# Order of work at six places of a hybrid transformer block on one core

## The chip, the core and the metric

The kernel runs on one core of a Trainium2 chip. The metric is the device time of one execution in microseconds, the median of three runs. All data are float32. PE is TensorE, DVE VectorE, ACT ScalarE, POOL GpSimd and SP SyncE, which only issues DMAs.

## The reference

One block of width 1024 over a sequence of 1024 tokens: a norm, a projection that feeds three mixers, an output projection with a residual, a second norm and a feed-forward part.

```python
h = rms_norm(x, attn_norm[l])
xa, qkv, z, b, a, c_q, c_kv, k_pe = jnp.split(h @ w_in[l], offsets, axis=-1)
y_a = pool_mixer(xa, pool_w[l], pool_scale[l])
y_b = gated_deltanet(qkv, z, b, a, dn_conv[l], dn_a_log[l], dn_dt_bias[l], dn_norm[l])
y_c = mla_attention(c_q, c_kv, k_pe, positions, ...)
x = x + jnp.concatenate([y_a, y_b, y_c], axis=-1) @ w_out[l]
h = rms_norm(x, mlp_norm[l])
x = x + jnp.square(jax.nn.relu(h @ w_up[l])) @ w_down[l]
```

`gated_deltanet` (4 heads of 128) solves, per chunk of 64 tokens, a unit lower triangular system and then carries a 128 x 128 state from chunk to chunk. `mla_attention` (4 heads) takes queries and keys from small latents, which are normed and rotated per token. `pool_mixer` takes moving means over 2 to 16 tokens.

## The kernel before

Every matmul is three (`mm3`, line 121): each operand is split into a high and a low part (`split`, line 113: ACT copies the high part, DVE or POOL subtracts), and high x high, high x low and low x high are added in PSUM. Tokens lie in eight tiles of 128 or two halves of 512.

The stages follow each other so:

- **First norms** (lines 196 to 260): eight x tiles are loaded, normed (`norm1`), transposed on PE (`turn`) and multiplied with a column group (`group`) that gives gates and latents. The weights of that group come in four loads (`load_g`) and are split by `split_g`. The order of SP is written by hand here; elsewhere a scheduler orders each engine's instructions by their place in the program and their dependences.
- **Column tiles** (`proj_tile`, line 480): the other columns of the projection in 18 tiles of 128, each in two halves of 24 matmuls. `tile_order` (line 473) is 6 to 9 (keys of the four heads), 0 and 1 (pool mixer), then per head query (2 to 5), value (10 to 13) and gate (14 to 17). `prefetch` loads and splits the next tile's weights. After each half, `pump(n, m)` (line 464) takes n steps of the generators in `side` and m of those in `slow`.
- Those generators are `latents()` (line 374: per token tile `latent_a`, `latent_b`, and `latent_c`, which norms and rotates), run during tiles 6 to 9; `lanes()` (line 575), the inverse of the triangular matrices in 31 steps of two DVE instructions, at high priority; `levels(h)`, which builds the larger blocks of the inverse with matmuls on PE after the small ones went through memory (`t_dram`); `chain(h)`, the state's way through the chunks of head h; and `pool(i, xa)`, the moving sums, on POOL.
- **Attention** (lines 990 to 1058): keys are loaded and transposed (`load_k`), then score, softmax and weighting pieces run while the chain of the last head ends: this beginning is the ramp.
- **Output projection** (`out_tile`, line 1088), per half of the tokens, with the squares for the second norm. `stats(hf)` (line 1112) sums them on PE, takes the reciprocal root on DVE, puts it on a diagonal (`dg`) and spreads it over the partitions with a matmul (line 1124).
- **Up part** (lines 1132 to 1413): a scheme of seven products (`products_12`, `product_6`, `products_rest`) for each of 16 pairs of weight blocks. `up_raw` loads the blocks, `halves` and `sums` combine them on POOL, `kept` combines the results and stores them in `u_dram`. Four pairs are begun early, during the output projection.
- **Down part** (`wave`, line 1359): seven products per group again, with `load_u`, `load_d`, `prepare`, and x loaded again from `x_dram`.

The last iteration over the pairs, where the up part turns into the down part, reads:

```python
        if last:
            kept(last, p - 1)
        if p == NFF // 2 - 1:
            load_u(0)
            load_u(1)
            load_d(0, 2, 0)
            acch = [S((P, 4, 1024), "H", 4)]
            prepare(0)
        products_rest(v, p)
        last = v
    kept(last, p)
```

## Time and profile before

| | us |
|---|---|
| runs | 1260.46, 1258.84, 1261.3 |
| profiled execution | 1258.98 |
| its span | 1257.3 |
| busy in the span: PE | 1178.5 (94%) |
| DVE | 851.7 (68%) |
| ACT | 575.0 (46%) |
| POOL | 260.9 (21%) |

The mean granted clock of PE is 0.972 of full speed. A span is from the first to the last instruction; an engine's busy time leaves out its waits. A window's row gives the same for a stretch of the span.

### The profile page before, as it was taken

Reading aid. Unit: us, or ns where it says so; the run is one execution under the profiler, and the core shown is the slowest. Engines: PE = TensorE matmul, PEld = TensorE weight load, DVE = VectorE, ACT = ScalarE, POOL = GpSimd, SP = SyncE. Lnnn points to the kernel's source line nnn. Section 1 sums busy time; section 2 is a strip of 40 time slices with the busy share of each in tenths; the row PEclk is TensorE's granted clock in tenths of the full one; section 3 lists DMA queues with packets and bytes.
Section 4 is the critical chain, followed back from the end, with each engine's and each line's share of the span. In section 5 each row is a group of like instructions: output and inputs, shape, how many; then the busy total and the mean of one; then the engine's idle time right before and its main releaser. Section 6 shows DMA issues by size and latency. Waiting matters only on the chain.

```text
span 1257.3 us, 16363 instructions
## 1 busy us (share of the span) xinstructions
PE 1178.5 (94%) x5802; PEld 965.9 (77%) x5802; DVE 851.7 (68%) x1692; ACT 575.0 (46%) x1187; POOL 260.9 (21%) x230
## 2 busy tenths in 40 slices
PE   5999996999999699997997999999997999999998
PEld 4968784788787578786876788888875888888887
DVE  7768779776657587538475556466457987786863
ACT  4655441554445477524264455555444333333330
POOL 3121023402020345243133323223210000000000
PEclk9999998999999699998999999999998999999999
DMA  6112222311101211571124443443489645442202
GB/s 251 35 51 89 92 89 84 109 33 29 36 24 55 89 34 35 188 248 66 42 76 167 167 162 124 176 150 136 176 318 382 207 163 167 151 135 93 100 27 101
DMA packets 84738, 152.62 MB, mean 121 GB/s; under 512 B 25520, under 2 KB 28720, under 8 KB 84656
## 3 DMA queue, kind: packets, MB, share of 16 engines
q1 hardware_dynamic: 74512, 140.03, 31.7%
q10 hardware_dynamic: 10144, 11.54, 2.7%
q8 instruction: 46, 0.75, 0.2%
q14 instruction: 36, 0.29, 0.1%
HBM read 105.41 MB, written 46.14 MB: 121 GB/s over the span
## 4 chain that ended last, share of the span: by engine, by line
PE 75%; DVE 12%; DMA 5%; ACT 3%; issue 2%; POOL 2%; SPq 0%; POOLq 0%; DVEq 0%; ACTq 0%
PE mm L1370 13%; PE mm L1154 11%; PE sm L1154 6%; PE sm L1370 5%; PE ch L1370 5%; PE mm L123 5%; PE mm L124 5%; PE mm L122 5%; PE ch L1154 2%; DMA upr<-in_w_up_dram 2%; PE sm L746 2%; PE ch L124 1%; DVE tl L587 1%; PE ch L122 1%; PE ch L123 1%
## 5 line engine op out<-in xcount | busy, mean ns | idle before, releaser
L1370 PE MATMUL mm<-dop,dop 128*128 128x512 f32 x768 | 180.2, 395 | 8.3 <-ACT dop L114 6.5
L1370 PEld LDWEIGHTS mm<-dop,dop 128*128 128x128 f32 x768 | 145.8, 190 | 40.8 <-ACT dop L114 7.3
L1154 PE MATMUL mm<-H,wop 128*128 128x512 f32 x576 | 137.4, 390 | 0.0
L1154 PEld LDWEIGHTS mm<-H,wop 128*128 128x128 f32 x576 | 107.9, 188 | 22.9 <-DVE wop L115 0.5
L114 ACT CAST dop<-wdr 128x1024 fp32r<-128x1024 f32 x48 | 50.4, 1049 | 164.0 <-PE ch L1370 69.8
L122 PE MATMUL mm<-H,w 128*128 128x512 f32 x288 | 117.4, 408 | 1.1 <-DVE t2k L501 1.1
L124 PE MATMUL mm<-H,w 128*128 128x512 f32 x288 | 116.5, 404 | 0.0
L123 PE MATMUL mm<-H,w 128*128 128x512 f32 x288 | 115.9, 402 | 0.0
L1154 PE MATMUL sm<-op,wop 128*128 128x512 f32 x384 | 94.9, 396 | 7.7 <-ACT wop L114 6.9
L1154 PEld LDWEIGHTS sm<-op,wop 128*128 128x128 f32 x384 | 72.7, 191 | 25.1 <-ACT wop L114 8.2
L115 POOL TENSOR_TENSOR w<-raw,w 128x1024 fp32r<-128x1024 f32 x18 | 43.8, 2431 | 229.4 <-ACT w L114 215.7
L115 DVE TENSOR_TENSOR dop<-wdr,dop 128x1024 fp32r<-128x1024 f32 x48 | 58.7, 1222 | 39.3 <-ACT dop L114 39.2
L1234 ACT ACTIVATE uo<-uo 128x512 f32<-128x512 f32 x48 | 30.3, 632 | 90.3 <-DVE uo L1212 46.0
L1370 PE MATMUL sm<-dop,dop 128*128 128x512 f32 x288 | 69.1, 395 | 2.4 <-ACT dop L114 2.0
L115 DVE TENSOR_TENSOR wop<-s,wop 128x512 fp32r<-128x512 f32 x64 | 47.6, 775 | 32.0 <-ACT wop L114 31.7
L115 DVE TENSOR_TENSOR dop<-H,dop 128x1024 fp32r<-128x1024 f32 x56 | 68.2, 1217 | 0.0
L1370 PE MATMUL ch<-dop,dop 128*128 128x512 f32 x288 | 67.8, 390 | 0.0
L1370 PEld LDWEIGHTS sm<-dop,dop 128*128 128x128 f32 x288 | 54.8, 191 | 14.7 <-ACT dop L114 2.5
L1370 PEld LDWEIGHTS ch<-dop,dop 128*128 128x128 f32 x288 | 54.2, 188 | 11.2
L122 PEld LDWEIGHTS mm<-H,w 128*128 128x128 f32 x288 | 54.8, 190 | 10.3 <-DVE t2k L501 1.5
L124 PEld LDWEIGHTS mm<-H,w 128*128 128x128 f32 x288 | 54.8, 190 | 9.4
L123 PEld LDWEIGHTS mm<-H,w 128*128 128x128 f32 x288 | 55.0, 191 | 9.0
(383 smaller groups left out, 2588.5 us busy)
## 6 DMA issues: line engine op xcount, KB each, us to landing
...
```

Of the source, the lines that this page charges most:

```text
L114: A.copy(hi, src)
L115: (eng or V).tensor_tensor(lo, src, f32(hi), op=ALU.subtract)
L122: PE.matmul(o, ah, bh, start=first, stop=False)
L123: PE.matmul(o, ah, bl, start=False, stop=False)
L124: PE.matmul(o, al, bh, start=False, stop=last)
L587: V.tensor_tensor(TL[:, j + 1:32, 0:m], TL[:, j + 1:32, 0:m], tv, op=ALU.subtract)
L746: PE.matmul(pa[:, c, :], lhs[:, c, :], rhs[:, c, :], start=True, stop=True)
L1154: PE.matmul(o, x_, y_, start=(first and j == 0 and q == 0), stop=(j == 3 and q == 2), skip_group_check=True)
L1234: A.activation(o, o, AF.Relu)
L1370: PE.matmul(o, x_[:, cs_], y_, start=(q in (0, 1, 3) and i == 0 and e == 0), stop=(i == GP - 1 and e == 2), skip_group_check=True)
```

## The change

- Start: all four weight loads come ahead of the second x tile, their splits are on DVE instead of POOL, and the norms of tiles 1 to 7 run in groups of two and three.
- Latents: the thirteen instructions of `latent_c` move from DVE to POOL, and `LAT` (steps per half) is 4.
- Column tiles: two gates come first, the mixer tiles last, with their second halves in `load_k` and in the ramp; a query's products with the keys stand between the halves of its value tile; three weight splits move to DVE.
- Norm statistics: `stats` ends with the reciprocal root; the diagonal and its matmul are `spread`, called one output tile later.
- Up part: each pair's blocks are loaded a pair ahead (`preload`).
- Turn: the first down weights and u blocks are loaded ahead of the kept stores; x is loaded again in four quarters by SP.

```diff
-LAT = 3
+LAT = 4
...
+SIDE = 9
...
     def load_g(q):
-        raw = wg_raw[q] = S((P, 2, NG), "raw", 3)
+        raw = wg_raw[q] = S((P, 2, NG), *(("raw", 3) if q < 3 else ("w", 4)))
         nc.sync.dma_start(raw, w_g[:, 2 * q:2 * q + 2, :])
 
     def split_g(q):
         wg_hi[q], wg_lo[q] = U((P, 2, NG), F32R, "wghi"), U((P, 2, NG), F32R, "wglo")
-        split(wg_hi[q], wg_lo[q], wg_raw.pop(q), G)
+        split(wg_hi[q], wg_lo[q], wg_raw.pop(q))
...
+    def norm1(*ts):
+        sl = slice(ts[0], ts[-1] + 1)
+        for t in ts:
+            A.activation(C((P, 1024), "lv", 3, BF16), xr[t], AF.Square, accum_out=ss1[:, t:t + 1])
...
+        for t in ts:
+            V.scalar_tensor_tensor(xr[t], xr[t], r1[:, t:t + 1], gbc, op0=ALU.mult, op1=ALU.mult)
...
@@ -225,31 +227,28 @@
     with tc.manual_schedule(engines={nc.sync.engine}):
         load_x()
         nc.sync.dma_start(gbc, attn_norm.broadcast_to([P, D]))
-        load_g(0)
+        for q in range(4):
+            load_g(q)
         load_x()
-        load_g(1)
-        load_g(2)
         load_x()
         norm1(0)
         split_g(0)
-        load_g(3)
+        split_g(1)
+        turn(0)
+        load_x()
         load_x()
         nc.sync.dma_start(par, params)
         nc.sync.dma_start(pos, positions)
-        turn(0)
-        split_g(1)
-        norm1(1)
         split_g(2)
         split_g(3)
         while len(xr) < NT:
             load_x()
-        for t in range(2, 1 + LEAD):
-            norm1(t)
         group(0)
+        norm1(1, 2)
         turn(1)
         for t in range(1, NT):
-            if t + LEAD < NT:
-                norm1(t + LEAD)
+            if t in (2, 4):
+                norm1(*range(t + 1, min(t + 4, NT) if t == 4 else t + 3))
...
         pe = C((P, 5, 32), "pe", 1)
-        V.tensor_tensor(pe[:, 0:4, :], q4[:, :, 64:96], rs[:, t, 4:8].unsqueeze(2).to_broadcast([P, 4, 32]), op=ALU.mult)
-        V.tensor_scalar(pe[:, 4, :], qk[:, 896:928], rs[:, t, 12:13], None, op0=ALU.mult)
-        V.tensor_tensor(pe, pe, pv("gpe").rearrange("p (a b) -> p a b", a=5), op=ALU.mult)
+        G.tensor_tensor(pe[:, 0:4, :], q4[:, :, 64:96], rs[:, t, 4:8].unsqueeze(2).to_broadcast([P, 4, 32]), op=ALU.mult)
+        G.tensor_scalar(pe[:, 4, :], qk[:, 896:928], rs[:, t, 12:13], None, op0=ALU.mult)
...
+        G.tensor_tensor(kn[:, :, 0:64], kv4[:, :, 0:64], rs[:, t, 8:12].unsqueeze(2).to_broadcast([P, 4, 64]), op=ALU.mult)
+        G.tensor_tensor(ro[:, :, 0:16], pe[:, :, 0:16], cb, op=ALU.mult)
+        G.tensor_tensor(ro[:, :, 16:32], pe[:, :, 16:32], cb, op=ALU.mult)
+        G.tensor_tensor(rt[:, :, 0:16], pe[:, :, 16:32], sb, op=ALU.mult)
+        G.tensor_tensor(rt[:, :, 16:32], pe[:, :, 0:16], sb, op=ALU.mult)
+        G.tensor_tensor(ro[:, :, 0:16], ro[:, :, 0:16], rt[:, :, 0:16], op=ALU.subtract)
+        G.tensor_tensor(ro[:, :, 16:32], ro[:, :, 16:32], rt[:, :, 16:32], op=ALU.add)
+        G.tensor_copy(qn[:, :, 64:96], ro[:, 0:4, :])
+        G.tensor_copy(kn[:, :, 64:96], ro[:, 4:5, :].to_broadcast([P, 4, 32]))
...
-    tile_order = [6, 7, 8, 9, 0, 1] + [b + h for h in range(H) for b in (2, 10, 14)]
+    tile_order = [6, 7, 8, 9, 14, 15, 2, 10, 3, 11, 4, 12, 16, 5, 13, 17, 0, 1]
...
-            loaded[ct] = load_w(w_tiles[ct], eng=G)
...
+            loaded[ct] = load_w(w_tiles[ct], eng=V if ct in (15, 2, 10) else G)
...
-
-    def conv_silu(ci, dst, after=None):
+            if between and hf == halves[0]:
+                between()
...
-    for i in range(2):
-        xa = U(s="xa")
+    XA = [None] * 2
+
+    def mixer(i):
+        xa = XA[i] = U(s="xa")
 
         def use_x(hf, pm):
             A.copy(xa[:, hf * 512:(hf + 1) * 512], pm)
 
-        proj_tile(i, use_x, 4, 3)
-        slow.append(pool(i, xa))
+        return i, use_x
...
+        proj_tile(2 + h, conv_silu(h, qt), SIDE)
+
+    def query_key(h):
+        qt = QT[h]
         transposed(qt, square_sums(ssq[:, h, :]))
...
     side.append(levels(0))
+    for h in range(2):
+        proj_tile(*gate(h), 8, 2)
     for h in range(H):
         queries(h)
-        v = values(h)
-        if h < H - 1:
-            proj_tile(*v, 6)
-            side.append(chain(h))
-            proj_tile(*gate(h), 6)
-        else:
-            z = gate(h)
-            proj_tile(*v, 6)
-            side.append(chain(h))
-            proj_tile(*z, 6, halves=(0,))
+        proj_tile(*values(h), SIDE, between=lambda: query_key(h))
+        side.append(chain(h))
+        if h > 1:
+            proj_tile(*gate(h), SIDE)
+    mix = [mixer(i) for i in range(2)]
+    for i in range(2):
+        proj_tile(*mix[i], SIDE, halves=(0,))
...
     for t in range(NT):
-        if t == 7:
-            proj_tile(*z, 6, halves=(1,), tag="mm")
+        if t == 0:
+            proj_tile(*mix[0], SIDE, halves=(1,))
+            slow.append(pool(0, XA[0]))
         load_k(t)
...
-    slow.append(pool_out(0))
-    slow.append(pool_out(1))
-    step(slow, 0)
+
+    def mixer_end():
+        proj_tile(*mix[1], 0, 0, halves=(1,), tag="ch")
+        slow.extend((pool(1, XA[1]), pool_out(0), pool_out(1)))
+        yield
...
+            if n == 0:
+                gens.append(mixer_end())
...
+    st = [None] * 2
+
     def stats(hf):
...
+        st[hf] = HM((P, 3, 4), s="st")
+        V.tensor_scalar(st[hf][:, 0, :], pt[:, :, 0], 1.0 / D, EPS, op0=ALU.mult, op1=ALU.add)
+        newton_rsqrt(st[hf][:, 1, :], st[hf][:, 0, :], st[hf][:, 2, :])
+
+    def spread(hf):
         dg = HM((P, 4, P), s="dg")
-        V.tensor_tensor(dg, ident.unsqueeze(1).to_broadcast([P, 4, P]), st[:, 1, :].unsqueeze(2).to_broadcast([P, 4, P]), op=ALU.mult)
+        V.tensor_tensor(dg, ident.unsqueeze(1).to_broadcast([P, 4, P]), st[hf][:, 1, :].unsqueeze(2).to_broadcast([P, 4, P]), op=ALU.mult)
         R[hf] = MM("ch")
         PE.matmul(R[hf], ones, dg.rearrange("p a b -> p (a b)"), start=True, stop=True)
...
+    raws = {}
+
+    def preload(p):
+        if p < NFF // 2 and p not in raws:
+            raws[p] = up_raw(p), up_raw(p + NFF // 2)
+
     def first_two(p):
         v = Pair()
-        v.r0 = up_raw(p)
+        preload(p)
+        v.r0 = raws[p][0]
         v.a11, v.a12 = w_op(v.r0[:, 0:4, :]), w_op(v.r0[:, 4:8, :])
...
             square(k, 1, n)
+            if n == 1:
+                spread(0)
...
-                    v.r0 = v.r1 = v.parts = v.s12 = None
+                    v.r0 = v.parts = v.s12 = None
                 else:
...
+        if p == 0:
+            spread(1)
     v0 = early_pairs[0]
     T2 = op_u()
...
+    raw_u = {}
+
     def load_u(n):
         g, q = divmod(n, 7)
-        if len(ur) < 2 and n % 2 == 0:
+        if n > 1 and len(ur) < 2 and n % 2 == 0:
             ur.append(S((P, 4, 2, 512), "H", 4))
         for h in range(2):
             p = GP * g + 2 * h
-            nc.sync.dma_start(ur[n // 2 % 2][:, 2 * (n % 2) + h], u_dram[q, p:p + 2].rearrange("a p t -> p a t"))
+            t_ = raw_u[n, h] = M((P, 2, 512), s="ur") if n < 2 else ur[(n // 2 - 1) % 2][:, 2 * (n % 2) + h]
+            nc.sync.dma_start(t_, u_dram[q, p:p + 2].rearrange("a p t -> p a t"))
+
+    def load_x(q):
+        hs = slice(512 * (q % 2), 512 * (q % 2) + 512)
+        nc.sync.dma_start(acch[q // 2][:, :, hs], x_dram[4 * (q // 2):4 * (q // 2) + 4, :, hs].rearrange("k p t -> p k t"))
...
             sums(v)
             products_12(v)
             product_6(v)
+        preload(p + 1)
+        if p == NFF // 2 - 1:
+            load_d(0, 2)
+            load_u(0)
+            load_d(0, 0)
+            load_u(1)
         if last:
             kept(last, p - 1)
         if p == NFF // 2 - 1:
-            load_u(0)
-            load_u(1)
-            load_d(0, 2, 0)
             acch = [S((P, 4, 1024), "H", 4)]
+            load_x(0)
             prepare(0)
         products_rest(v, p)
         last = v
+    load_d(0, 1, 3)
     kept(last, p)
+    acch.append(S((P, 4, 1024), "H", 4))
     load_u(2)
-    acch.append(S((P, 4, 1024), "H", 4))
-    for k in range(KD):
-        x2[k] = acch[k // 4][:, k % 4, :]
-        nc.scalar.dma_start(x2[k], x_dram[k])
-    load_d(0, 1, 3)
+    load_x(2)
     load_u(3)
+    load_x(3)
+    load_x(1)
     for n in range(n_wave):
         g, q = divmod(n, 7)
         if n + 1 < n_wave:
```

POOL, ahead of the inverse; `tl` is its start value, `w` a weight tile's low part, `nrm`, `ro` and `pe` belong to latents. Before:

```order
L115 TENSOR_TENSOR w_1792<-raw_1789,w_1791 128x1024
L115 TENSOR_TENSOR w_1959<-raw_1956,w_1958 128x1024
L578 MEMSET tl_1774 128x1024
L579 AFFINE_SELECT tl_1774<-tl_1774 128x1024
L115 TENSOR_TENSOR w_2061<-raw_2058,w_2060 128x1024
L115 TENSOR_TENSOR w_2265<-raw_2262,w_2264 128x1024
L115 TENSOR_TENSOR w_2435<-raw_2432,w_2434 128x1024
L621 COPY xs_1945<-xa_1696 128x1
L622 TENSOR_TENSOR xs_1945<-xa_1696 128x1023
```

With the change (line numbers are those of the changed kernel):

```order
L358 TENSOR_TENSOR nrm_1804<-qk_1625,rs 128x4x64
L359 TENSOR_TENSOR nrm_1804<-qk_1625,rs 128x4x64
L366 COPY nrm_1804<-ro_1805 128x4x32
L367 COPY nrm_1804<-ro_1805 128x4x32
L579 MEMSET tl_1819 128x1024
L580 AFFINE_SELECT tl_1819<-tl_1819 128x1024
L116 TENSOR_TENSOR w_2245<-raw_2242,w_2244 128x1024
L116 TENSOR_TENSOR w_2394<-raw_2391,w_2393 128x1024
```

The two rows of `tl` (memset and identity) came behind a weight split and ahead of three; now they come behind the last latent.

DVE, norm statistics of the first half; `st` is the reciprocal root, `dg` the diagonal, `wop<-s` the split of a summed weight block, `x<-mm` the residual addition of an output tile. Before:

```order
L115 TENSOR_TENSOR wop_6146<-upr_6141,wop_6146 128x512
L132 SCALAR_TENSOR_TENSOR st_5853<-st_5853 128x4
L133 SCALAR_TENSOR_TENSOR st_5853<-st_5853 128x4
L1122 TENSOR_TENSOR dg_5866<-ident,st_5853 128x512
L115 TENSOR_TENSOR wop_6154<-s_1193_6151,wop_6154 128x512
L1128 SCALAR_TENSOR_TENSOR x_1117_5544<-x_1117_5544,g_5525,ch_5868 128x512
L1128 SCALAR_TENSOR_TENSOR x_1118_5546<-x_1118_5546,g_5525,ch_5868 128x512
```

With the change (line numbers are those of the changed kernel):

```order
L116 TENSOR_TENSOR wop_6100<-upr_6093,wop_6100 128x512
L133 SCALAR_TENSOR_TENSOR st_5805<-st_5805 128x4
L134 SCALAR_TENSOR_TENSOR st_5805<-st_5805 128x4
L116 TENSOR_TENSOR wop_6106<-s_1193_6103,wop_6106 128x512
L1105 TENSOR_TENSOR x_1139_5676<-mm_5819,x_1139_5676 128x512
L1136 TENSOR_TENSOR dg_5849<-ident,st_5805 128x512
L1142 SCALAR_TENSOR_TENSOR x_1117_5496<-x_1117_5496,g_5477,ch_5851 128x512
```

The diagonal moved behind the split of a summed block and one residual addition.

SP's queue, first pairs of the up part; `upr` are weight blocks of pairs 1, 2, 3, `uo` and `t` results that are stored. Before:

```order
L1230 DMA u_dram<-uo_6307 128x512
L1230 DMA u_dram<-uo_6339 128x512
L1142 DMA upr_6545<-in_w_up_dram 128x1024
L1142 DMA upr_6547<-in_w_up_dram 128x1024
L1230 DMA u_dram<-uo_6499 128x512 x2
L1230 DMA u_dram<-t_1247_6567 128x512
L1230 DMA u_dram<-t_1248_6568 128x512
L1230 DMA u_dram<-t_1247_6567 128x512
L1230 DMA u_dram<-t_1248_6568 128x512
L1142 DMA upr_6640<-in_w_up_dram 128x1024
L1142 DMA upr_6642<-in_w_up_dram 128x1024
```

With the change (line numbers are those of the changed kernel):

```order
L1251 DMA u_dram<-uo_6259 128x512
L1156 DMA upr_6437<-in_w_up_dram 128x1024
L1251 DMA u_dram<-uo_6291 128x512
L1156 DMA upr_6439<-in_w_up_dram 128x1024
L1156 DMA upr_6519<-in_w_up_dram 128x1024
L1156 DMA upr_6521<-in_w_up_dram 128x1024
L1251 DMA u_dram<-uo_6455 128x512 x2
L1251 DMA u_dram<-t_1249_6523 128x512 x2
L1251 DMA u_dram<-t_1250_6524 128x512 x2
L1156 DMA upr_6614<-in_w_up_dram 128x1024
L1156 DMA upr_6616<-in_w_up_dram 128x1024
```

The blocks of the second of these pairs moved ahead of the six stores that follow, those of the third one group of stores up.

## Rows read from the trace of the kernel before

**Rows 1.** Waits of PE: engine, line, releaser: us in total, times, longest.
```profile
PE sm L519 <- DVE qt L509: 12.4, 1, 12.4
```

**Rows 2.** Windows: us, busy (instructions) of five engines, PEclk, DMA share, GB/s.
```profile
0.00:20.00 20.00, 4.86 (x14) 3.55 (x15) 12.60 (x34) 10.02 (x15) 10.55 (x36) 1.00 0.75 267
62.00:157.00 95.00, 91.99 (x435) 72.73 (x434) 72.90 (x247) 48.68 (x146) 16.42 (x13) 0.98 0.23 77
204.00:228.00 24.00, 10.68 (x45) 8.70 (x44) 24.00 (x64) 4.88 (x19) 11.20 (x12) 0.64 0.23 88
407.00:443.00 36.00, 24.70 (x101) 18.09 (x101) 20.14 (x62) 15.13 (x47) 12.33 (x20) 0.67 0.26 86
566.00:581.00 15.00, 8.22 (x22) 5.60 (x22) 12.07 (x25) 6.74 (x11) 4.13 (x4) 0.66 0.26 101
655.00:694.00 39.00, 31.34 (x126) 23.82 (x125) 20.66 (x28) 17.93 (x32) 13.05 (x10) 0.96 0.43 155
694.00:917.00 223.00, 222.18 (x979) 183.41 (x978) 125.63 (x164) 120.33 (x213) 70.88 (x48) 1.00 0.42 154
926.00:974.00 48.00, 37.34 (x139) 28.12 (x138) 30.83 (x34) 20.55 (x24) 0.00 (x0) 0.89 1.00 385
```

**Rows 3.** Timeline of POOL and DVE, first norms: start, us, instruction.
```profile
11.23 5.84 POOL L115 TENSOR_TENSOR wglo<-raw,wghi 128x848 fp32r<-128x848 f32 x3 [7.80 <-ACT wghi L114]
...
11.55 1.68 DVE L131 TENSOR_TENSOR t<-r 128x1 f32<-128x1 f32 x1
...
15.20 1.89 DVE L133 SCALAR_TENSOR_TENSOR r<-t,r 128x1 f32<-128x1 f32 x1
17.13 0.16 DVE L131 TENSOR_TENSOR t<-r 128x1 f32<-128x1 f32 x1
```

**Rows 4.** Timeline of DVE, then of POOL, during the inverse.
```profile
199.12 2.11 DVE L587 TENSOR_TENSOR tl<-tl,lt 128x255 f32<-128x255 f32 x1
...
203.52 0.41 DVE L587 TENSOR_TENSOR tl<-tl,lt 128x256 f32<-128x256 f32 x1
...
204.85 0.21 DVE L367 COPY nrm<-ro 128x128 f32<-128x128 f32 x1
...
207.99 0.41 DVE L360 TENSOR_TENSOR nrm<-qk,rs 128x256 f32<-128x256 f32 x1
...
199.05 1.90 POOL L622 TENSOR_TENSOR xs<-xa 128x1023 f32<-128x1023 f32 x1
...
203.58 0.43 POOL L627 TENSOR_TENSOR yp<-xs,xa 128x16 f32<-128x16 f32 x1
```

**Rows 5.** Timeline of SP's queue, the finished inverse.
```profile
227.27 0.32 SPq L591 DMA_DIRECT2D t_dram<-tl  x1
229.90 0.81 SPq L730 DMA_DIRECT2D lv<-t_dram  x2
```

**Rows 6.** Timeline of DVE, then of PE, norm statistics.
```profile
566.74 0.69 DVE L115 TENSOR_TENSOR wop<-s,wop 128x512 fp32r<-128x512 f32 x1 [4.10 <-ACT wop L114]
...
572.35 1.64 DVE L1122 TENSOR_TENSOR dg<-ident,st 128x512 f32<-128x512 f32 x1
574.12 0.69 DVE L115 TENSOR_TENSOR wop<-s,wop 128x512 fp32r<-128x512 f32 x1
...
574.14 2.05 PE L1124 MATMUL ch<-dg,ones 128*128 128x512 f32 x2 [6.78 <-DVE dg L1122]
```

**Rows 7.** Timeline of SP's queue, early pairs.
```profile
664.97 0.96 SPq L1142 DMA_DIRECT2D upr<-in_w_up_dram  x2
...
680.05 0.91 SPq L1142 DMA_DIRECT2D upr<-in_w_up_dram  x2
```

**Rows 8.** Timeline of SP's queue, then of ScalarE's, turn to the down part.
```profile
922.90 2.65 SPq L1338 DMA_DIRECT2D wdr<-in_w_down_dram  x4
...
946.29 5.70 SPq L1338 DMA_DIRECT2D wdr<-in_w_down_dram  x4
...
940.52 9.06 ACTq L1413 DMA_DIRECT2D H<-x_dram  x5
```

More of the change, by code (lines that the diff above doesn't have):

```diff
@@ L477, in prefetch, with proj_tile @@
         if ct not in loaded:
-            loaded[ct] = load_w(w_tiles[ct], eng=G)
-    def proj_tile(ct, use, n=0, m=1, halves=(0, 1), tag="mm"):
+            loaded[ct] = load_w(w_tiles[ct], eng=V if ct in (15, 2, 10) else G)
+    def proj_tile(ct, use, n=0, m=1, halves=(0, 1), tag="mm", between=None):
         prefetch(ct)
@@ L1176, in halves @@
     def halves(v, p):
-        r0, r1 = v.r0, up_raw(p + NFF // 2)
-        v.r1 = r1
+        preload(p)
+        r0, r1 = raws.pop(p)
         v.s12 = M((P, 2, 4, P), s="s12")
@@ L1353, in prepare @@
             split(o[0], o[1], wr[g, (2, 0, 0, 1, 4, 3, 2)[q], h])
-            split(o[2], o[3], ur[n // 2 % 2][:, 2 * (n % 2) + h])
+            split(o[2], o[3], raw_u.pop((n, h)))
             ops[n].append(o)
@@ L1373, in wave @@
             hs = slice(512, 1024) if q in (3, 4, 6) else slice(0, 512)
[L1374 removed]
+            x_ = acch[k // 4][:, k % 4, hs]
             V.tensor_tensor(x_, o, x_, op=ALU.add)
```

26 lines of the change are left out of this document (4 added, 22 removed).

## Prediction

> **What bounds the kernel now.** I read the table of PE's waits first, then the windows by stage, then the timelines at the six places. In each window row the reader is to see two numbers: the length less PE's busy time is idle, and PE's busy time multiplied by one less the granted clock is what the clock takes. From [rows 2]:
>
> - start, 0 to 20: idle 15.1 us
> - tiles 6 to 9, 62 to 157: idle 3.0, clock 1.8
> - inverse, 204 to 228: idle 13.3, clock 3.8
> - attention ramp, 407 to 443: idle 11.3, clock 8.2
> - norm statistics, 566 to 581: idle 6.8, clock 2.8
> - early pairs, 655 to 694: idle 7.7, clock 1.3
> - turn to the down part, 926 to 974: idle 10.7, clock 4.1
>
> That is 67.9 us idle and 22.0 us of clock. Where PE sat idle the clock went from 2.4 to 1.2 GHz: the means of 0.64 to 0.67 in three rows lie between these levels. The row 694 to 917 shows the rest: 222.18 of 223 us busy, 0.227 us for each of its 979 matmuls. PE is the bound, and no matmul is removed. So the change can win only from these 89.9 us.
>
> **First norms.** POOL's three weight splits take 5.84 us from 11.23, and beside them three operations of one column take 1.68 to 1.89 us each on DVE, and 0.16 once POOL is done [rows 3]: 5 us lost. On DVE a split of 512 columns takes 0.69 us [rows 6], so one of 848 some 1.15; two of them, 2.3 us, now stand ahead of the first transposed split. Against this, two more weight loads (0.43 MB each) pass x1 and x2 on SP: at the window's 267 GB/s [rows 2] x1 comes up to 3.2 us later, and group 0 is what PE does meanwhile. I take -1.5 us, between -3 and +1.
>
> **Latents on GpSimd.** DVE sheds thirteen instructions per token tile. They run from 0.2 to 0.41 us, the 256-column one at 0.41 [rows 4], about 3.5 us a tile and 28 us for eight. POOL has two prices: 0.43 us for 16 columns and 1.90 for 1023 [rows 4], so some 0.41 + 1.46 ns a column. The thirteen hold 1568 columns: 7.6 us a tile and 61 for eight, an estimate that I take; 28 if POOL were as fast as DVE. In 62 to 157 POOL is busy for 16.4 of 95 us [rows 2], so it fits: 77. What hides it is that nothing of PE reads a latent before the attention. What loses the cover: the identity for the inverse is made by POOL behind the last latent (order rows of POOL). In the tile stage I take 0: DVE, 72.9 of 95 us busy, gets lighter by up to four tiles (14 us), but short POOL operations may hold it. Bounds -2 and +6 (holds of 42 us on DVE: 72.9 - 14 + 42 = 101).
>
> **Tile order and inverse.** PE waits 12.4 us for the query of head 0 [rows 1] because DVE works through the 62 operations of the inverse. It is busy for 24.00 of 24.00 us there [rows 2], and an inverse step that takes 0.41 us takes 2.11 beside a POOL addition of 1.90 us [rows 4]. Mixer additions (POOL) and latents (DVE) both leave this place. Against that, levels of head 0 must still wait. After tile 15 the order of PE has seven half-tiles, 24 x 0.227 = 5.44 us each, 38 us, ahead of the first product with the inverse. The inverse needs at most 62 x 0.41 = 25 us alone. DVE's ordinary work for seven halves is 38 x 0.77 = 29 us by its share in 62 to 157; if half of it stands between, 40, and with three POOL weight splits beside it, each good for a hold of up to 2 us, 38 to 45 (estimates). Then comes the way through memory: stored at 227.27, read back from 229.90 on [rows 5], about 5 us with the landing (an estimate). The product is ready at 43 to 50, PE at 38: a wait of 5 to 12 in place of 17.1 us. I take -6, the cautious end. Bounds: -14 (a wait of 3), +6 (the inverse starts ten late behind POOL's last latent).
>
> **Attention ramp.** Half a tile (5.44 us) is moved into the chain's idle time; it comes out of a place where PE was busy, so it counts one to one, unless the ramp's end is set by the chain itself. Less idle gives back part of the 8.2 us of clock. Against it: the second mixer's additions, four of about 1.9 us on POOL [rows 4], now stand between the attention's normalisations there. I take -7. Bounds -16 (all but a sixth of the 19.5) and 0 (the additions cost what the matmuls bring).
>
> **Norm statistics.** The spread matmul waits 6.78 us for the diagonal [rows 6]. The edit puts 11 more matmuls ahead of it (31 instead of 20: 2.5 us). But DVE's order moves as well: the diagonal, which ran from 572.35, now comes behind a weight split that ran at 574.12 and behind the addition of the next output tile. 574.12 + 0.69 + 0.69 = 575.5, and with 0.7 to 1.64 of its own the diagonal ends at 576.2 to 577.1, 2 to 3 us later. That split hangs on a chain that the edit leaves alone: the one before it, at 566.74, ended 4.10 us in which DVE stood waiting for ScalarE [rows 6], which gets its input from POOL and POOL from a load. So the 2.5 us of cover are given back: idle is 6.8 again, and the clock falls again. I take -1. Bounds -6 (the split comes early because its load does) and +2.
>
> **Early pairs.** The loads of pair 2 were issued at 664.97 and of pair 3 at 680.05, each behind four stores that wait for DVE [rows 7]. Now pair 2's are issued together with pair 1's, pair 3's behind the first group of stores (at about 665). Each is then on the chip a pair (some 15 us) before it is summed. What these two pairs cost goes, with its clock. What pair 1 costs stays: its second load keeps its place, and two more loads share the queues with it. Of 9.0 us I take -6.5. Bounds -9 and -2 (pair 1's sums come 4 us later).
>
> **Turn.** Three waits: the first down weights, issued at 922.90; the second ones, issued at 946.29 behind stores that wait for DVE; ScalarE, which stands for 9.06 us at issuing five x loads before its next cast [rows 8]. After: the first weights go ahead of the last kept stores but one, behind one 1 MB load of x, so some us earlier; the second ones take about the place that the first had, 23 us earlier; x is loaded by SP, in quarters, as the waves need it. The queues carry 385 GB/s through this window at a busy share of 1.00 [rows 2]; 3 of the 4 MB of x (8 us at that rate) leave the front of it. I take -10 of 14.8. Bounds -14 and -3 (the bytes alone set the end).
>
> **The sum** is -1.5 + 0 - 6 - 7 - 1 - 6.5 - 10 = -32 us on the profiled execution, whose time of 1258.98 us is 1.5 below the median: 1227 there, 1228.5 for the median.
>
> **A rule against it.** A step of the inverse beside POOL's addition took 2.11 us and not 0.41, and ended with it [rows 4]. The Trainium skill, "SBUF — State Buffer", section "Who interferes with whom", says that a VectorE instruction with two SBUF inputs and a GpSimd instruction that reads SBUF lock each other out for a whole instruction, whichever starts second. The trace agrees for this pair. By that rule the move trades 28 us of VectorE for up to 61 us in which it may be locked out, and the sum would be the first rival's.
>
> **Rivals.**
> 1. GpSimd's latents hold VectorE. Of 72.9 us in 62 to 157, 14 go and 28 to 61 of holds come: 87 to 120 us in a window of 95, so up to 25 lost; at 54, 18. With the other terms 1228.5 + 18 = 1246.5. For: the held steps. Against: many of DVE's operations there read PSUM, and a short POOL operation holds for less than a long one. 0.16.
> 2. Everything works: the inverse is ready in time, the ramp fills, the diagonal comes early. Then 60 of the 89.9 us go: 1200. For: nothing but order stands against it. Against: seven halves of cover for 43 to 50 us, and DVE's order at the diagonal. 0.10.
> 3. Slower. The place is POOL's queue ahead of the inverse. If its latents take not 7.6 us a tile but 13 (if VectorE holds each of the thirteen for 0.41 us, as long as its own 256-column row), the inverse starts 8 x 5.4 = 43 us later than I reckoned, PE stands all that time, and the clock falls. From 7.6 + 32 / 8 = 11.6 us a tile on this eats the whole sum. At 13: 1228.5 + 43, and some 3 for the clock, about 1274. 0.08.
> 4. No change: several edits do not do what they say, as at the diagonal, and the turn stays bound by its bytes: about 1260. 0.04.
>
> **Chances.** The forecast, 20 to 45 us saved, has 0.62. Two tenths of a per cent, 2.5 us, is about what a measurement can tell. Faster: 0.62 + 0.16 + 0.10 = 0.88; same 0.04; slower 0.08. The terms' bounds, taken as independent, give some 15 us either way; upwards it must take in the middle of rival 1. Range 1209 to 1249.
>
> **What would show it.** Right: no wait of PE for the query; one of 5 to 12 us for the inverse's products; a clock of 0.9 or more in the ramp; a wait for the diagonal as long as before; the sums of pairs 2 and 3 not waiting for a load; ScalarE not issuing loads at the turn. Wrong: DVE over 90 us busy in the tile stage, latents of over 8 us a tile on POOL, or a wait for the diagonal that is gone.

## The result, and the profile after

The changed kernel takes 1244.63 us, the median of 1246.92, 1244.36, 1244.9 and 1242.77, against 1259.65 for the kernel before (four runs, 1256.61 to 1261.3). The ratio is 0.9884, 95% interval 0.9858 to 0.991: some 15 us are won. The profiled execution's span is 1245.1 us, against 1257.3. PE is busy for 1177.1 us (before 1178.5), DVE for 858.9 (851.7), POOL for 292.1 (260.9); the mean granted clock is 0.971 (0.972). The time lies in the forecast range, but the forecast gain of 32 us was more than twice what came.

The waits of PE in the changed kernel, as engine, line and releaser: us in total, times, longest:

```profile
PE sm L751 <- DMA lv<-t_dram: 13.9, 1, 13.9
PE sm L178 <- DVE x L204: 10.2, 2, 9.2
PE ch L1138 <- DVE dg L1136: 5.8, 1, 5.8
PE s L926 <- ACT H L937: 4.9, 1, 4.9
PE sm L957 <- POOL pr L943: 4.1, 2, 3.0
PE ch L836 <- DVE lv L832: 3.7, 2, 2.3
PE ch L836 <- DMA lv<-t_dram: 3.0, 1, 3.0
PE mm L1168 <- DVE uo L1233: 3.0, 2, 2.3
```

The wait for the query [rows 1] is gone. One of 13.9 us for the first product with the inverse (L751) has come. The one for the diagonal (L1138) stays. L178 is the start, L926 and L957 are the ramp, L836 is the chain of the heads, L1168 the up part.

The windows of the changed kernel, stage by stage: start and end, us, then busy us (instructions) of PE, PEld, DVE, ACT and POOL, PEclk, DMA share, GB/s:

```profile
0.00:20.00 20.00, 8.88 (x32) 7.41 (x33) 12.59 (x40) 10.69 (x16) 2.70 (x32) 1.00 0.88 308
62.00:157.00 95.00, 91.14 (x438) 70.94 (x437) 66.17 (x202) 48.87 (x151) 44.17 (x89) 1.00 0.23 77
204.00:236.00 32.00, 17.66 (x118) 14.89 (x117) 20.27 (x44) 6.57 (x15) 4.41 (x4) 0.68 0.27 72
236.00:420.00 184.00, 175.09 (x1108) 141.46 (x1107) 122.78 (x373) 87.26 (x290) 24.93 (x18) 0.95 0.12 32
420.00:470.00 50.00, 38.39 (x184) 28.91 (x183) 25.24 (x41) 26.30 (x61) 30.46 (x39) 0.76 0.31 104
571.00:592.00 21.00, 14.97 (x66) 11.55 (x65) 9.82 (x25) 6.19 (x11) 6.75 (x6) 0.84 0.42 137
660.00:700.00 40.00, 37.86 (x166) 30.55 (x165) 34.11 (x40) 21.71 (x40) 18.23 (x12) 1.00 0.48 173
700.00:920.00 220.00, 217.72 (x954) 179.77 (x953) 149.61 (x164) 117.06 (x209) 74.16 (x46) 0.99 0.41 152
920.00:960.00 40.00, 40.00 (x179) 33.10 (x177) 29.90 (x35) 17.98 (x23) 0.00 (x0) 1.00 0.91 332
```

The window of the heads' tiles in the kernel before, which the prediction did not read:

```profile
230.00:408.00 178.00, 173.80 (x1182) 142.21 (x1180) 118.23 (x342) 91.19 (x274) 24.14 (x19) 1.00 0.17 44
```

Loss is again idle plus PE's busy time by one less the clock, from these rows and [rows 2]:

| stage | loss before | loss after | difference | forecast |
|---|---|---|---|---|
| start | 15.1 | 11.1 | -4.0 | -1.5 |
| tiles 6 to 9 | 4.8 | 3.9 | -0.9 | 0 |
| inverse | 17.1 | 20.0 | +2.9 | -6 |
| heads' tiles | 4.2 | 17.7 | +13.5 | no term |
| ramp | 19.5 | 20.8 | +1.3 | -7 |
| norm statistics | 9.6 | 8.4 | -1.2 | -1 |
| early pairs and what follows to 917 or 920 | 9.8 | 6.6 | -3.2 | -6.5 |
| turn | 14.8 | 0.0 | -14.8 | -10 |

The differences add up to -6.4 us and the spans differ by 12.2; the rest is in stretches outside these windows or in PE's busy time. The pattern is plain all the same: the start and the turn won more than was forecast, the early pairs half of it, and the middle lost.

**Why the inverse is late.** SP's queue in the changed kernel, start, us, instruction:

```profile
173.25 0.34 SPq L369 DMA_DIRECT2D n_dram<-nrm  x1
173.65 0.42 SPq L562 DMA_DIRECT2D a_dram<-at  x1
177.86 0.32 SPq L369 DMA_DIRECT2D n_dram<-nrm  x1
178.27 0.38 SPq L447 DMA_DIRECT2D raw<-in_w_tiles_dram  x1
178.75 1.15 SPq L565 DMA_DIRECT2D lanes<-a_dram  x2
...
216.24 0.33 SPq L592 DMA_DIRECT2D t_dram<-tl  x1
```

The same place in the kernel before:

```profile
164.97 0.32 SPq L561 DMA_DIRECT2D a_dram<-at  x1
167.59 0.77 SPq L564 DMA_DIRECT2D lanes<-a_dram  x2
```

The matrices (`at`) went to memory as soon as DVE had made them, and back 2.6 us later. Now the store of a latent that POOL still works on stands ahead of each of the two steps: `at` is complete at 169.33 (DVE L561: 167.18 plus 2.15), its store starts at 173.65, and the load back, behind another latent's store at 177.86 and a weight load, at 178.75. DVE and POOL in the changed kernel (timeline, with the idle time before an instruction in brackets):

```profile
178.56 2.31 DVE L502 SCALAR_TENSOR_TENSOR t2k<-mm,cw,t2k 128x511 f32<-128x511 f32 x3 [5.29 <-ACT t2k L499]
...
184.14 0.69 DVE L586 TENSOR_TENSOR lt<-lanes,tl 128x31 f32<-128x31 f32 x1 [3.20 <-DMA lanes<-a_dram]
...
193.50 2.35 DVE L588 TENSOR_TENSOR tl<-tl,lt 128x192 f32<-128x192 f32 x1
...
193.25 2.39 POOL L116 TENSOR_TENSOR w<-raw,w 128x1024 fp32r<-128x1024 f32 x1 [8.46 <-ACT w L115]
```

The first step runs at 184.14, 14.8 us after `at`. The queue is the smaller part of that: DVE stands for the load only from 180.9 on, 3.20 us. Ahead of the first step it has three steps of a query's convolution (L502), for which it stands 5.29 us until ACT has made their input, and which end at 180.87. In the kernel before, the first step came 7.65 us after `at` (172.60 against 164.95). Once begun, the inverse takes 32.1 us, to 216.2, and PE gets its first product at 222.50. It had run out of other work at 208.6. In the kernel before, the inverse took 54 us (172.60 to 226.7), with eight steps of 1.9 to 2.6 us instead of two (193.50 and 204.34): moving work away from it did shorten it. An inverse step beside a weight split on POOL again takes as long as the split, 2.35 beside 2.39 us. That agrees with the rule of the Trainium skill, "SBUF — State Buffer", section "Who interferes with whom", which the prediction cites.

**Why the heads' tiles lose.** POOL, then DVE, in the changed kernel:

```profile
328.16 0.94 POOL L742 MEMSET tt<- 128x1024 f32 x1
...
327.13 2.00 DVE L129 TENSOR_SCALAR sr<-sv 128x4 int32<-128x4 int32 x1
...
350.68 2.26 DVE L133 SCALAR_TENSOR_TENSOR sw<-sw,sv 128x4 f32<-128x4 f32 x1
...
371.96 2.29 DVE L133 SCALAR_TENSOR_TENSOR sw<-sw,sv 128x4 f32<-128x4 f32 x1
```

These are steps of four columns of the chain's reciprocal root, 0.16 or 0.17 us elsewhere. The first ends at 329.13, when POOL's memsets behind the weight split end (328.16 plus 0.94); the other two began during a weight split on POOL (350.55 and 371.86, plus 2.38) and ended with it. Behind them PE waits at L836 for 3.0, 1.4 and 2.3 us. The table of waits puts the 3.0 us down to a load (`lv<-t_dram`), but the matmul at L836 reads a tile that DVE's L832 writes, and in `e4_pool_dve` below the same wait of 3.0 us, behind the same held step, is put down to L832. The idle time in this window is 8.9 us against 4.2 before. The larger part of the loss is the clock, which drops behind idle spells of 1.3 to 3 us: 0.95 over 175.09 busy us makes 8.8 of the 17.7. That part is not the tile order's alone: in `e1_store_pool`, with the same order, the clock in this window is 0.99, and in `e9_ff_start_spread`, with the order of before, it is 0.96 from 230 to 408.

**Why the ramp does not gain.** DVE, then ACT, then POOL, in the changed kernel:

```profile
449.73 1.56 DVE L629 SCALAR_TENSOR_TENSOR yp<-xs,rw,xa 128x1008 f32<-128x1008 f32 x1 [6.82 <-POOL xs L623]
...
447.19 1.04 ACT L621 COPY xs<-xs 64x1024 f32<-64x1024 f32 x1 [4.09 <-POOL xs L623]
...
448.94 0.89 ACT L937 ACTIVATE H<-s,stt 128x768 f32<-128x768 f32 x1
...
447.38 2.32 POOL L623 TENSOR_TENSOR xs<-xs 64x1016 f32<-64x1016 f32 x1
```

The second mixer's sums run on POOL until 449.7. Two engines have a step of that mixer ahead of the softmax: ACT its copy (L621) ahead of the exponentials (L937) that PE waits for, DVE its last step (L629) ahead of the next maximum (L934). So ACT stands for 4.09 us, PE for 4.9 (L926 in the table of waits) and DVE for 6.82: not the 1.9 us of one addition, but the whole row of them in one stretch.

### The profile page after: what moved, and what is told of

It is laid out like the page before. It is cut to its first block, busy times and chain, and to the rows that moved or that the text cites. A ratio compares the mean times of both kernels' runs of the same rounds, so it can differ in the third digit from the quotient of the medians.

```text
span 1245.1 us, 16313 instructions
## 1 busy us (share of the span) xinstructions
PE 1177.1 (95%) x5802; PEld 966.1 (78%) x5802; DVE 858.9 (69%) x1547; ACT 570.5 (46%) x1187; POOL 292.1 (23%) x327
## 4 chain that ended last, share of the span: by engine, by line
PE 72%; DVE 12%; POOL 4%; DMA 4%; ACT 4%; issue 3%; SPq 0%; POOLq 0%; DVEq 0%; ACTq 0%
PE mm L1402 14%; PE mm L1168 12%; PE sm L1168 6%; PE ch L1402 5%; PE sm L1402 5%; PE mm L125 4%; PE mm L124 4%; PE mm L123 4%; PE ch L1168 3%; DMA upr<-in_w_up_dram 2%; PE sm L751 2%; PE ch L125 1%; DVE tl L588 1%; PE ch L123 1%; PE ch L124 1%
## 5 line engine op out<-in xcount | busy, mean ns | idle before, releaser
L1402 PE MATMUL mm<-dop,dop 128*128 128x512 f32 x768 | 176.0, 389 | 0.0
L1168 PE MATMUL mm<-H,wop 128*128 128x512 f32 x576 | 139.2, 394 | 3.0 <-DVE uo L1233 3.0
L1168 PEld LDWEIGHTS mm<-H,wop 128*128 128x128 f32 x576 | 108.9, 190 | 27.1 <-DVE uo L1233 4.0
L123 PE MATMUL mm<-H,w 128*128 128x512 f32 x280 | 116.3, 415 | 0.2 <-DVE zs L710 0.2
L125 PE MATMUL mm<-H,w 128*128 128x512 f32 x280 | 115.2, 411 | 0.0
L124 PE MATMUL mm<-H,w 128*128 128x512 f32 x280 | 114.3, 408 | 0.0
L1168 PE MATMUL sm<-op,wop 128*128 128x512 f32 x384 | 92.4, 389 | 1.4 <-ACT p L1231 1.4
L116 POOL TENSOR_TENSOR w<-raw,w 128x1024 fp32r<-128x1024 f32 x15 | 36.5, 2433 | 221.9 <-ACT w L115 191.7
L1168 PEld LDWEIGHTS sm<-op,wop 128*128 128x128 f32 x384 | 72.0, 188 | 16.8 <-ACT p L1231 1.9
L116 DVE TENSOR_TENSOR wop<-s,wop 128x512 fp32r<-128x512 f32 x64 | 44.1, 704 | 38.4 <-ACT wop L115 38.4
L116 DVE TENSOR_TENSOR dop<-H,dop 128x1024 fp32r<-128x1024 f32 x52 | 63.2, 1215 | 0.0
L502 DVE SCALAR_TENSOR_TENSOR t2k<-mm,cw,t2k 128x511 f32<-128x511 f32 (+2 forms) x72 | 53.4, 742 | 11.7 <-ACT t2k L499 11.4
L1205 POOL TENSOR_TENSOR s<-upr 128x512 f32<-128x512 f32 x16 | 24.1, 1504 | 159.2 <-DVE uo L1194 73.5
L125 PEld LDWEIGHTS mm<-H,w 128*128 128x128 f32 x280 | 54.0, 193 | 9.1
```

The lines of the kernel that those rows point to most:

```text
L116: (eng or V).tensor_tensor(lo, src, f32(hi), op=ALU.subtract)
L123: PE.matmul(o, ah, bh, start=first, stop=False)
L124: PE.matmul(o, ah, bl, start=False, stop=False)
L125: PE.matmul(o, al, bh, start=False, stop=last)
L502: V.scalar_tensor_tensor(acc[:, s:], pm[:, :512 - s], w, acc[:, s:], op0=ALU.mult, op1=ALU.add)
L1168: PE.matmul(o, x_, y_, start=(first and j == 0 and q == 0), stop=(j == 3 and q == 2), skip_group_check=True)
```

## The experiments

Gains are one less the ratio, times 1259.65 us. The kernels fall into two kinds: parts of the change put into the kernel before (e6 to e10, e12), and parts undone or mended in the changed one (e1 to e4).

| kernel | median, us | ratio [95%] | gain, us |
|---|---|---|---|
| the change | 1244.63 | 0.9884 [0.9858, 0.991] | 14.6 |
| e6_ff_only | 1230.75 | 0.977 [0.9746, 0.9795] | 29.0 |
| e7_ff_start | 1224.73 | 0.9726 [0.969, 0.9761] | 34.5 |
| e9_ff_start_spread | 1226.07 | 0.9729 [0.971, 0.9748] | 34.1 |
| e8_ff_start_latents | 1236.42 | 0.9801 [0.9762, 0.9841] | 25.1 |
| e2_latents_dve | 1246.79 | 0.9905 [0.9867, 0.9943] | 12.0 |
| e10_gates_first | 1263.69 | 1.0033 [1.002, 1.0046] | -4.2 |
| e12_sums_later | 1229.01 | 0.9752 [0.9738, 0.9765] | 31.2 |
| e1_store_pool | 1239.19 | 0.9845 [0.9811, 0.9879] | 19.5 |
| e1b_store_pool_ident | 1242.25 | 0.9852 [0.982, 0.9884] | 18.6 |
| e3_spread_later | 1242.6 | 0.9848 [0.9811, 0.9885] | 19.1 |
| e4_pool_dve | 1239.46 | 0.9823 [0.9782, 0.9864] | 22.3 |

**The queue ahead of the inverse.** `e1_store_pool` is the changed kernel with the latents' store on the queue of the engine that makes them:

```diff
-        nc.sync.dma_start(n_dram[t], nm_)
+        G.dma_start(n_dram[t], nm_)
```

> The changed kernel, but each latent's store goes through POOL's queue instead of SP's. Queue theory: in the changed kernel SP's store of latent 6 (173.25) stood ahead of the last block of the triangular matrices (ready at 169.3, stored at 173.65), and the store of latent 7 (177.86) ahead of its load for the inverse (178.75). Without them the inverse starts 3 to 5 us earlier than 184.1 (then the identity, which POOL finishes at 180.0, is the limit), PE's wait of 13.9 us for the inverse falls to 9 to 11, and the whole is 3 to 6 us under the changed kernel: 1239 to 1242. Rival, the held VectorE: the inverse is late because POOL's latents hold DVE; then its start and the wait stay within 1 us, 1244 to 1246.

`e1b_store_pool_ident` makes the inverse's start value (memset and identity) ahead of the latents as well:

```diff
+    TL = U((P, 32, 32), s="tl")
+    G.memset(TL.rearrange("p a b -> p (a b)"), 0.0)
...
     def lanes():
-        TL = U((P, 32, 32), s="tl")
```

> As the kernel with the stores on POOL's queue, and the identity for the inverse is made ahead of the latents. Queue theory: now only the data decide, the inverse starts at 176 to 178, 6 to 8 us earlier than in the changed kernel, PE's wait falls to 6 to 8 us, 1236 to 1239. Rival (DVE held): no further change against the kernel with only the stores moved.

SP's queue, then DVE, in `e1_store_pool`:

```profile
170.69 0.34 SPq L562 DMA_DIRECT2D a_dram<-at  x1
...
173.98 0.69 SPq L565 DMA_DIRECT2D lanes<-a_dram  x2
...
179.23 2.32 DVE L502 SCALAR_TENSOR_TENSOR t2k<-mm,cw,t2k 128x511 f32<-128x511 f32 x3 [5.73 <-ACT t2k L499]
181.46 0.18 DVE L586 TENSOR_TENSOR lt<-lanes,tl 128x31 f32<-128x31 f32 x1
```

The matrices leave at once, and the load back is 4.8 us earlier than in the changed kernel. But the first step runs at 181.46, only 2.7 us earlier, and the inverse ends at 216.5, no earlier than in the changed kernel: PE waits 11.9 us at L751 instead of 13.9. The 5 us won are measured with intervals that overlap. The limit that both expectations name, the identity on POOL (done at 180.9 in `e1_store_pool`), is not the one: in `e1b_store_pool_ident` it is made early, and the first step still runs at 181.62 (wait 11.7). In both kernels it comes right behind the convolution steps, for which DVE stands 5.7 us until ACT has made their input, and ACT 9 us until PE has ended that half tile. So the queue's order did delay the inverse's start, by some 3 us; the rest is the place of the first step on DVE, behind a tile that PE has not done. No run here moves the step to another place, so that this would bring the wait down is not shown.

**The parts alone.** `e6_ff_only` puts the edits of the up part and of the turn into the kernel before (`preload`, `load_x`, the order of `load_d` and `load_u`, as in the diff of the change):

```diff
+        preload(p + 1)
+        if p == NFF // 2 - 1:
+            load_d(0, 2)
+            load_u(0)
```

> The kernel before, with the edits of the up part and the turn alone (loads a pair ahead, first down weights and u blocks ahead of the stores, x in quarters by SP). If the changed kernel's gain is all of it, and what the start brought was lost again between 185 and 470: the windows give 3.1 us for the early pairs and 15.3 for the turn, so 18 us under before, 1240 to 1243, faster than the changed kernel. Rival: the parts depend on each other (the turn gains only because what lies ahead of it came earlier), gain 10 to 15, 1245 to 1250.

The last pairs and the turn in its windows (columns as above):

```profile
650.00:694.00 44.00, 39.85 (x174) 31.97 (x173) 36.19 (x37) 23.87 (x44) 22.61 (x15) 1.00 0.45 161
694.00:917.00 223.00, 223.00 (x986) 184.65 (x985) 146.30 (x160) 119.58 (x211) 72.15 (x44) 1.00 0.45 164
917.00:960.00 43.00, 43.00 (x191) 35.63 (x190) 41.79 (x49) 20.55 (x24) 0.00 (x0) 1.00 0.97 360
```

Nothing is lost at the turn, and 4.2 us in the early pairs. These edits alone bring 29 us, twice the whole change and 11 more than was expected of them. The windows show 14.8 of it at the turn, 5.6 in the early pairs and 2.6 at the norm statistics, where this kernel has no edit (560 to 584: 24 us less 19.73 busy at a clock of 0.86, so 7.0 lost for 9.6 before). Where the other 6 are is not shown. `e7_ff_start` adds the edits of the start:

```diff
-        split(wg_hi[q], wg_lo[q], wg_raw.pop(q), G)
+        split(wg_hi[q], wg_lo[q], wg_raw.pop(q))
...
-        load_g(0)
+        for q in range(4):
+            load_g(q)
```

> The kernel before with the edits of the up part, the turn and the start (first norms, weight splits of the group on DVE). If the start's gain is its own, the 3.7 us that the windows of the first 62 us showed come on top of the kernel with the up part and turn alone (1230.75): 1226 to 1228.5. Rival: group 0 earlier only moves the wait to the later norms or the first tile's weights, 1229.5 to 1231.5.

It brings 34.5 us, the most of all kernels here; the start's share of some 5.5 (2 to 5 were expected) is not clear of the noise, as the intervals overlap. `e9_ff_start_spread` adds `spread` to that:

```diff
+            if n == 1:
+                spread(0)
...
+        if p == 0:
+            spread(1)
```

> The kernel before with the edits at the start, in the feed-forward part, and with the split of the norm statistics into stats and spread; no edit in the tile stage, the inverse or the ramp. The same without the statistics' edit took 1224.7 us (ratio 0.9726). Theory A (the statistics' edit brings what its window showed in the changed kernel, 2.6 us of idle and clock, most of it clock, although the wait for the diagonal stays at about 5 us): 1222 us, ratio 0.970 to 0.972, PE waits 4 to 6 us for the diagonal. Rival B (the gain there came from the other edits, through what ScalarE and POOL have left over when the output projection begins): 1224 to 1226 us, ratio 0.972 to 0.974.

It changes nothing that can be measured (0.9729 against 0.9726), as its rival B had it, and PE still waits 3.9 us for the diagonal. `e8_ff_start_latents` is `e7_ff_start` with `latent_c` on POOL and `LAT` 4, in the old tile order:

```diff
-LAT = 3
+LAT = 4
...
-        V.tensor_copy(qn[:, :, 64:96], ro[:, 0:4, :])
+        G.tensor_copy(qn[:, :, 64:96], ro[:, 0:4, :])
```

> As the kernel with up part, turn and start, and the latents on POOL with four steps per half; tiles in the old order. Theory A, the loss of the changed kernel between 185 and 460 comes from the new tile order and ramp, not from the latents: DVE is relieved of 14 us while it works on the inverse, PE's wait of 12.4 us for the first query falls to 3 to 8 us, 1218 to 1223. Theory B, the latents are the loss (their stores stand ahead of the inverse's data on SP, POOL holds DVE): the wait grows or stays, 1227 to 1235.

SP's queue in it:

```profile
171.35 0.42 SPq L560 DMA_DIRECT2D a_dram<-at  x1
178.74 0.33 SPq L447 DMA_DIRECT2D raw<-in_w_tiles_dram  x1
179.16 0.69 SPq L563 DMA_DIRECT2D lanes<-a_dram  x2
```

Latents and `LAT` together cost 9.4 us here by the ratios; no run separates the two. PE's wait for the query falls from 12.4 to 8.6 us, but PE's idle time from 160 to 250 is the same (15.8 and 15.7 us); the clock there is 0.89 and not 0.92, and where the 9.4 us lie is shown only in part. The load back follows the store by 7.8 us, where it was 2.6 in the kernel before: a weight load, whose buffer a POOL split frees at 178.7, stands ahead of it, and DVE stands 5.57 us for the load ahead of the first step. The matrices themselves are complete 9 us later than in `e7_ff_start` (167.8 against 158.8). The inverse ends at 229.9, there at 221.1. `e2_latents_dve` is the changed kernel with the latents back on DVE, all thirteen as in

```diff
-        G.tensor_copy(qn[:, :, 64:96], ro[:, 0:4, :])
+        V.tensor_copy(qn[:, :, 64:96], ro[:, 0:4, :])
```

> The changed kernel with the latents back on DVE. Theory A: order of tiles and ramp lose, so nothing comes back: PE still waits 12 us or more for the inverse, 1243 to 1249. Theory B: the latents on POOL lose, the inverse starts at 175 to 178 and the wait falls under 8 us, 1236 to 1240.

That wins nothing back: 12.0 us against 14.6, and PE still waits 10.9 us at L751, with no latent on POOL. Its matrices come 7 us later (176.2 against 169.3), behind latents on DVE, so in this order the latents on POOL had a use. With the latents on DVE, the tile stage's other edits (tile order, ramp, `LAT` and `SIDE`, splits on DVE) cost 34.1 - 12.0 = 22 us, counted from `e9_ff_start_spread`.

**The tile order by itself.** `e10_gates_first` is `e7_ff_start` with two gates ahead of the first query and the mixer whole at its old place:

```diff
-    tile_order = [6, 7, 8, 9, 0, 1] + [b + h for h in range(H) for b in (2, 10, 14)]
+    tile_order = [6, 7, 8, 9, 0, 1, 14, 15, 2, 10, 3, 11, 4, 12, 16, 5, 13, 17]
...
+    for h in range(2):
+        proj_tile(*gate(h), 8, 2)
```

> The kernel before with the edits at the start and in the feed-forward part, and of the tile stage's edits only the order of the column tiles with two gates ahead of the first query; the pool mixer's tiles stay where they were, behind the keys, whole; latents stay on VectorE; the ramp is the one of before. It has eleven half tiles ahead of the first product with the inverse instead of seven. Without the tile order it took 1224.7 us (ratio 0.9726). Theory A (the new order's loss in the heads' tiles comes from the mixer having left them: nothing stands any more between the chain's steps, and its sums block POOL and VectorE in the ramp): PE's wait for the query of 12.4 us goes, none of over 3 us comes for the inverse, and the time falls by 5 to 12 us to 1213 to 1220, ratio 0.963 to 0.969. Rival B (two gates first are the loss themselves: levels, chain and weights of the heads come later and meet POOL's weight splits): the wait moves to the first levels or to the chain, the time is 1222 to 1235, ratio 0.970 to 0.981.

PE in it, then DVE:

```profile
213.03 0.77 PE L122 MATMUL mm<-H,w 128*128 128x512 f32 x1 [22.06 <-DVE zs L703]
...
212.21 0.68 DVE L703 SCALAR_TENSOR_TENSOR zs<-t2k,mm 128x512 f32<-128x512 f32 x1
```

Neither theory named this. The time is 39 us above that of `e7_ff_start`. PE stands for 22.06 us, not for the inverse's result but for a bank of PSUM: a gate's last step (L703) reads PSUM on DVE and comes behind the steps of the inverse there, and until it has run PE cannot begin the tile that takes its bank. Of the 39 us the windows, read as above, show some 12 more lost at this place than in `e7_ff_start` (186 to 236), 9 in the heads' tiles and 13 in the ramp; the causes of the last two stay open. In this order gates are no cover for the inverse, which fills DVE; a mixer tile, which ACT alone reads out (`A.copy`), does not wait for DVE.

**POOL beside the inverse.** `e12_sums_later` is `e7_ff_start` with the mixer's sums put off:

```diff
-        slow.append(pool(i, xa))
+        XA.append(xa)
...
             proj_tile(*gate(h), 6)
+            if h < 2:
+                slow.append(pool(h, XA[h]))
```

> The kernel before with the edits at the start and in the feed-forward part, tile order, latents and ramp as before, and one edit of its own: the moving sums of the pool mixer are put off until the gate tiles of heads 0 and 1, so that they no longer run on POOL beside the inverse. Without that edit it took 1224.7 us (ratio 0.9726), and PE waited 12.4 us for the query of head 0 while four additions of 1.9 to 2.05 us held steps of the inverse. Theory A (what makes the inverse late beside work that PE has in hand is VectorE's instructions being held by POOL's long ones): four holds of some 1.6 us go, the wait for the query falls to 5 to 8 us, the time by 4 to 8 us to 1217 to 1221, ratio 0.966 to 0.970. Rival B (the inverse is bound by its own 62 steps and by the latents that stand between them, and the sums hold the chain's steps where they are now): the wait stays at 10 us or more, or what it loses comes back as waits for the chain at the later place, 1223 to 1230 us, ratio 0.971 to 0.977.

The wait for the query in `e7_ff_start`, and then in `e12_sums_later`:

```profile
PE sm L517 <- DVE qt L507: 12.4, 1, 12.4
```

```profile
PE sm L517 <- DVE qt L507: 5.5, 1, 5.5
```

Windows of `e7_ff_start` at the inverse and in the heads' tiles (columns as above):

```profile
196.00:232.00 36.00, 20.31 (x104) 15.58 (x102) 31.91 (x75) 8.66 (x27) 16.11 (x17) 0.81 0.31 102
232.00:404.00 172.00, 168.35 (x1155) 138.10 (x1153) 115.80 (x344) 88.80 (x271) 23.26 (x17) 1.00 0.16 42
```

The same in `e12_sums_later`:

```profile
196.00:232.00 36.00, 26.76 (x167) 21.91 (x165) 25.71 (x76) 12.47 (x38) 6.38 (x7) 0.86 0.33 101
232.00:404.00 172.00, 166.92 (x1088) 135.78 (x1085) 116.20 (x328) 85.72 (x258) 35.26 (x30) 0.98 0.16 42
```

The holds at the inverse are real: without the sums the wait falls by 6.9 us, as theory A had it, and the loss there by 6.5 (19.5 to 13.0). But 4.7 us come back at the heads' tiles (3.7 to 8.4), where POOL now has 35.26 us of work and not 23.26, and 1.8 in the ramp (404 to 446: 18.0 to 19.8). The edit is right at its place and worth nothing in all, as rival B had it. That the additions hold DVE at the later place too is not shown: DVE's busy time there rises by 0.4 us only, and 3.3 of the 4.7 are the clock.

**The ramp and the statistics.** `e4_pool_dve` is the changed kernel with the moving sums on DVE, in four lines as in

```diff
-            G.tensor_tensor(nxt[rows, s:], cur[rows, s:], cur[rows, :1024 - s], op=ALU.add)
+            V.tensor_tensor(nxt[rows, s:], cur[rows, s:], cur[rows, :1024 - s], op=ALU.add)
```

> The changed kernel with the mixer's moving sums on DVE instead of POOL. If these sums on POOL (1.85 to 2.3 us each, between the normalisations of the attention at 436 to 450) are what makes PE wait in the ramp for ScalarE's scores (4.9 us) and POOL's normalisation (4.1 us), both waits fall under 1 us and the clock comes back sooner: 1234 to 1238. Rival: the ramp is set by the chain of the last head, the waits only change their names: 1243 to 1246.

The ramp in its windows:

```profile
420.00:470.00 50.00, 44.64 (x252) 34.77 (x252) 42.04 (x71) 33.80 (x79) 28.64 (x31) 0.90 0.33 105
```

The loss in the ramp halves, from 20.8 to 5.4 + 4.5 = 9.9 us, and the wait of 4.9 us at L926 is gone, so the mixer's tail on POOL caused about half of it. The gain over the changed kernel, 7.7 us by the ratios, is less and its interval overlaps. `e3_spread_later` calls `spread(0)`, and the first normed tiles, one output tile later still:

```diff
-            if n == 1:
+            if n == 2:
                 spread(0)
-            if n in (1, 2):
+            if n in (2, 3):
```

> The changed kernel, with the diagonal and its matmul two output tiles after the statistics instead of one, and the norms of the first eight blocks one tile later. If the wait of 5.8 us is set by the split on DVE that stands ahead of the diagonal, then 24 more matmuls (5.4 us) hide nearly all of it and keep the clock: 5 to 7 us under the changed kernel, 1238 to 1240. Rival: the wait moves on to the splits of the normed blocks or to the products behind them, gain under 2 us, 1243 to 1245.

The wait in its place:

```profile
PE ch L1129 <- ACT sq L1116: 3.8, 1, 3.8
```

The wait for the diagonal is gone and one for ACT's squares has come, so moving the matmul only moves the wait, as the rival had it. The time is the changed kernel's within the interval.

## Why the prediction was right or wrong

The sum failed in its middle. For latents, inverse, ramp and statistics it had -14 us, where the windows show +2.1; and the heads' tiles, at +13.5, had no term. By place:

- **Turn**: right in mechanism, the term too small: -14.8 against -10. The step that failed is "3 of the 4 MB of x (8 us at that rate) leave the front of it", with the rest still bound by bytes: they did not bound it at all. The queues run at a share of 0.91 and PE is busy for 40.00 of 40 us.
- **First norms**: -4.0 against -1.5, outside the bound of -3. PE's busy time in the first 20 us rose from 4.86 to 8.88. Three loads pass x1, not the two that were counted; still PE waits only 1.0 us for it (L178, the lesser of its two waits), so the late x tile, to which half of the gain was given, cost less than reckoned.
- **Early pairs**: right direction, half the size: -3.2 against -6.5. The waits for loads went; what came in their place is a wait for DVE's `uo` (L1168, 3.0 us in all).
- **Norm statistics**: the order was read rightly: the diagonal still waits 5.8 us, behind the split and the addition. The -1.2 is not the edit's, though: `e6_ff_only` gains 2.6 there without it, and `e9_ff_start_spread` nothing with it.
- **Latents**: 0 taken in the tile stage, -0.9 measured. On POOL they take 5.65 us a tile (45.2 us in all over its thirteen rows) against an estimate of 7.6; DVE's busy time there falls by 6.7 us, not 14. What failed is the list of what they could delay: I named the identity behind the last latent, which held nothing, but not their stores on SP, which stand ahead of the inverse's store and load. Rival 1 put its price into the tile stage; with `LAT` they do cost 9.4 us by `e8_ff_start_latents`, but not there: from 62 to 157 PE is busy for 91.11 of 95 us in it, and for 91.89 in `e7_ff_start`.
- **Tile order and inverse**: +2.9 against -6. Failed step: "The product is ready at 43 to 50" counted from a first step at once after the matrices. It began 14.8 us after them; 7.65 of these could be read in the kernel before, and of the rest the queue has some 3 us. The inverse's own length, 32.1 us, was below the 38 to 45 reckoned, and the way through memory 6.3 us against 5. So the product came 14.8 + 32.1 + 6.3 = 53.2 us after the matrices, and PE's cover ended after 39.3.
- **Heads' tiles**: no term; +13.5. A changed order of tiles moves weight splits, loads and chain steps against one another everywhere, and I costed only its first place. 4.7 of it are idle time; the 8.8 of clock differ between executions.
- **Ramp**: +1.3 against -7, beyond the bound of 0. The additions were priced singly; the order on ACT and DVE, which puts steps of the mixer ahead of the softmax, was not read there.

So the terms for start, pairs and turn (-18) were too small, -22 by the windows and 34.5 us by runs, and those for the middle (-14) had the wrong sign, by runs 20 us lost. That the time lies in the range is luck: one error covered half of the other. Of the signs named, none of the three for wrong came; of those for right, two failed: the wait for the inverse, 13.9 and not 5 to 12 us, and the clock in the ramp, 0.76 and not 0.9. What stays open is how those 22 us split between tile order and ramp: the ramp alone was not tried, `e10_gates_first` meets a wait that the change, with its mixer moved, does not have, and the clock's part in the heads' tiles is not the same in each execution. The best kernel measured keeps the start, up part and turn and drops the rest: 1224.73 us.
